# Weights written as pairs of keys in two halves of a row, and 32-column squares read at every second column, in a one-core hybrid attention layer

## The chip, the core and the metric

The kernel runs on one core of a Trainium2 chip. The metric is the device time of one execution in microseconds (us); lower is better. Three timed executions of the kernel before gave 795.85, 797.52 and 797.86 us, so the median is 797.52 us. The profile is of a fourth execution, which took 796.99 us.

## What is computed

One layer of a streaming encoder, for a prompt of 1024 tokens and a sample of 32 tokens that share all weights. Of the reference, cut to what matters here:

```python
u = rmsnorm(h, g_pre) @ w_in                     # qA kA vA gA qB kB vB gB, 512 columns each
oA = band_attention(...)                         # 8 heads x 64, softmax over own 64-frame chunk and 8 before
oB = stick_breaking(...)                         # 8 heads x 64, strictly causal
y  = concat(oA * silu(gA), oB * silu(gB)) @ w_out
h  = h + rmsnorm(y, g_post)
h  = h + sigmoid(h @ w_ple_gate) * (p @ w_ple)

# band attention:        s = q k^T * scale + bias;  w = softmax(s);  o = w v
# stick breaking:        z = q k^T * scale
#   log_1m = log_sigmoid(-z) (causal);  after = sum of log_1m over later keys
#   w = exp(log_sigmoid(z) + after);    o = w v
```

Both attentions make a matrix of weights with queries in the 128 partitions and keys along the row. The product with the values needs it the other way round, with keys in the partitions. How the weights are turned is what the change touches.

## The kernel before

**Stages.** The 16 heads are taken in pairs of heads, in the order A0 B0 A1 B1 A2 B2 A3 B3 (`pairs`). While the attention of one pair runs, the projections of the next are woven between its steps, and during B3 the eight gate projections. After the attention come two 1024-wide products (output and gate), done with a seven-product scheme. All matrix products are split in high and low parts (`hi`, `lo`).

**Order.** All operations are first recorded, then a planner (`Recorder.plan`) sets the order on each engine from modelled costs, and `emit` (line 497, which is why every row of the profile says L497) issues them. Each engine then executes its own queue strictly in that order: TensorE (PE), VectorE (DVE), ScalarE (ACT), GpSimd (POOL), and SyncE (SP), which issues all DMAs.

**A head, block by block.** A head has eight query blocks of 128 (`i` = 0 to 7). `scores(i)` multiplies q and k into PSUM (tile `SA` or `SB`). In band attention (A), VectorE adds the bias and takes the row's extreme (`om<-SA,biasA`, with its result in `statA`), then ScalarE takes the exponential with the row sum (`be<-om,statA`, followed by a short accumulator read into `sums`). In stick breaking (B), ScalarE takes a sigmoid (`om<-SB`), VectorE scans it (`om<-om,SB`), and GpSimd subtracts neighbours (`be<-om`). `om` and `be` are two ring buffers in SBUF. So the weights `be` have two producers: **ScalarE's exponential in A, GpSimd's difference in B**.

**Turning the weights.** Most blocks are small and are turned on TensorE (`ptw`). The blocks in the table `ROUND` go another way: A blocks 4, 5, 6, 7 (640 keys each) and B blocks 4, 5, 6 (640, 768, 896 keys), 4 x 8 + 3 x 8 = 56 in all. For them, `weights_t` has VectorE turn 32x32 squares (`STREAM_TRANSPOSE om<-be`), then one DMA writes the row to DRAM (`swapA<-om`, `swapB<-om`) and one brings it back turned (`be<-swapA`, `be<-swapB`). ScalarE then makes the high part (`wTh<-be`) and VectorE the low part (`wTl<-be,wTh`).

For this, the key of a square's row has to be dealt out by four: the producer's helper `apart` (line 872) writes key 4k + c of each 128-key block to column 32c + k, so that consecutive results are written 32 columns apart, and one square is 32 consecutive columns. The values are turned in a like way in `values_out` (line 731), which reads every second column of its source: `vxA<-stvA`, `vxB<-stvB`, 128x1024 each. `keys_out` turns the keys from consecutive columns (`ktB<-stkB`, 128x1024).

**Row sums.** After A's block 7, VectorE inverts the eight sums (`sumsA<-sumsA`), TensorE turns them (`ptsA<-ident,sumsA`) and ScalarE copies them out (`sumrowA`). This transpose stands at a fixed place in TensorE's queue, and whatever is behind it there waits until block 7's exponential is done.

Of the kernel before, what the change touches and what calls it, by code (L numbers as in the profile page):

```python
# [13 lines left out]
P = 128  # L14
# [28 lines left out]
def f(ap):  # L43

    return ap.bitcast(F32)
# [457 lines left out]
def stream_step(  # L503
# [7 lines left out]
    nc = rec  # L511
# [8 lines left out]
    def psum(tag, name):  # L520
        return ps.tile([P, 512], F32, tag=tag, name=name, bufs=PS_BUFS[tag])

    def scratch(shape, name):
        return Buf(shape, F32, name=name, real=dram.tile(shape, F32, tag=name, name=name))
# [28 lines left out]
        out=maskb, in_=maskb, pattern=[[-1, P]], base=0, channel_multiplier=1,  # L553
# [282 lines left out]
    def attention(ab, p, h):  # L836
# [14 lines left out]
        def lo_block(i):  # L851
            return max(0, i - 4) if ab == "A" else 0
# [4 lines left out]
        def cost(i):  # L857
            return i + 1 - lo_block(i)
# [13 lines left out]
        def apart(i, x, out=False):  # L872

            if i not in together:
                return x
            return x.rearrange("p (b c k) -> p b k c" if out else "p (b k c) -> p b k c", c=4, k=32)

        def scores(i):
            L, kd, kl = Lq[h], KDh[h], KLD[h]
# [13 lines left out]
            if ab == "B":  # L893
                a, b, s = pieces[-1]
                dg = s[:, b - a - P:b - a]
                nc.vector.tensor_tensor(dg, dg, maskb, ALU.add)
                nc.gpsimd.memset(w0[:, n:n + 1], 1.0)
                for a, b, s in pieces:
                    nc.scalar.activation(w0[:, a:b], s, AF.Sigmoid, scale=-1.0)
                for a, b, s in reversed(pieces):  # L900
                    rev = w0[:, a:b][:, ::-1]
                    nc.vector.tensor_tensor_scan(rev, rev, s, w0[:, b:b + 1], ALU.mult, ALU.bypass)
                nc.gpsimd.tensor_tensor(apart(i, w1[:, 0:n], True), apart(i, w0[:, 1:n + 1]), apart(i, w0[:, 0:n]), ALU.subtract)
            else:
                m = small.tile([P, 4], F32, tag="stat", name=f"stat{nm}_{i}", bufs=6)
                sums = box["sums"]
                for j, (a, b, s) in enumerate(pieces):
                    nc.vector.tensor_tensor_reduce(
                        w0[:, a:b], s, box["bias"][:, n - b:n - a][:, ::-1], 1.0,
                        3e38 if j == 0 else m[:, j - 1:j], ALU.add, ALU.min, m[:, j:j + 1])  # L910
                last = len(pieces) - 1
                nc.scalar.activation(apart(i, w1[:, 0:n], True), apart(i, w0[:, 0:n]), AF.Exp, bias=m[:, last:last + 1], scale=-1.0, accum_out=sums[:, i:i + 1])
                if i == 7:
                    nc.vector.reciprocal(sums, sums)
                    pt = psum("T", f"pts{nm}")
                    nc.tensor.transpose(pt[0:8, 0:P], sums, ident)
                    row = at.tile([P, 4 * P], F32, tag="ot", name=f"sumrow{nm}", bufs=2)[0:8, 0:P]
                    nc.scalar.copy(row, pt[0:8, 0:P])
                    dma(rs_dr[2 * p + h, 0:SEQ].rearrange("(i q) -> i q", q=P), row)
# [8 lines left out]
        def weights_t(i):  # L928
            g = i // 4
            step, size = LAID[ab, g]  # L930
            if g not in wT:
                wT[g] = [x.tile([P, size * P], f"{x.name}{nm}_{g}") for x in (ringh, ringl)]
            b0 = lo_block(i)
            w0, w1 = state.pop(i)
            n = i + 1 - b0
            at_ = ((i - 4 * g) * step + b0) * P
            hi, lo = (x[:, at_:at_ + n * P] for x in wT[g])
            if i in together:

                group = together[i]  # L940
                done_with.append((i, hi, lo))
                if i != group[-1]:
                    return
                w0, w1 = whole[group]
                m = sum(cost(x) for x in group)
                first = {x: sum(cost(y) for y in group[:k]) for k, x in enumerate(group)}
                squares = w0[:, 0:m * P].rearrange("p (c b q) -> p b c q", c=4, q=32)
                for x, _, _ in done_with:
                    y = slice(first[x], first[x] + cost(x))
                    nc.vector.transpose(squares[:, y], w1[:, y.start * P:y.stop * P])  # L950
                dr = scratch([4, P, m * 32], f"swap{nm}_{i}")
                dma(dr.rearrange("g (k c) x -> (g k) (c x)", c=4), w0[:, 0:m * P])
                dma(w1.rearrange("p (g x) -> p g x", g=4), dr.rearrange("g p x -> p g x"))
                turned = w1.rearrange("p (g b q) -> p g b q", g=4, q=32)
                for x, hi, lo in done_with:
                    src = turned[:, :, first[x]:first[x] + cost(x), :]
                    hi, lo = (y.rearrange("p (b g q) -> p g b q", g=4, q=32) for y in (hi, lo))
                    nc.scalar.copy(hi, src)
                    nc.vector.tensor_tensor(lo, src, f(hi), ALU.subtract)
                done_with.clear()  # L960
                return
            for b in range(0, n, 4):
                m = min(4, n - b)
                pt = psum("T", f"ptw{nm}_{i}_{b}")
                for x in range(m):
                    nc.tensor.transpose(pt[:, x * P:(x + 1) * P], w1[:, (b + x) * P:(b + x + 1) * P], ident)
                c = slice(b * P, (b + m) * P)
                nc.scalar.copy(hi[:, c], pt[:, 0:m * P])
                nc.vector.tensor_tensor(lo[:, c], pt[:, 0:m * P], f(hi[:, c]), ALU.subtract)
# [25 lines left out]
        out = {("B",): (0.0, begin)}  # L995
        for i in range(8):
            out["S", i] = (0.107 * cost(i) + SPACE_S, lambda i=i: scores(i))
            out["T", i] = (0.107 * cost(i) + SPACE_T, lambda i=i: weights_t(i))
# [255 lines left out]
    for n in range(-1, 8):  # L1254
        a = len(order)
        if n < 7:
            ab, p = pairs[n + 1]
# [458 lines left out]
    def short_product(nm, left, q):  # L1716
        o1, o2, both, minus = left
        acc = psum("S", f"{nm}8_{q}")[0:2 * NS]
        todo = ((o1, "B11"), (o2, "B21")) if q == 0 else ((both, "B22"), (minus, "T3"))
        i = 0  # L1720
        for a, key in todo:
            for kt in range(KT):
                for part in range(2):
                    nc.tensor.matmul(acc, a[:, kt, :], blocks[nm, key][:, part, kt, :], start=(i == 0), stop=(i == 4 * KT - 1))
                    i += 1
        y = at2.tile([P, 512], F32, tag="bias", name=f"{nm}j8_{q}", bufs=2)
        nc.scalar.copy(y[0:NS], acc[NS:2 * NS])
        nc.vector.tensor_tensor(y[0:NS], acc[0:NS], y[0:NS], ALU.add)
        return y[0:NS]
# [31 lines left out]
    for m, (nm, src, group) in enumerate(sets):  # L1761
        last_set = m == len(sets) - 1
        state = [{}, {}]
        for n, prod in enumerate(ORDER):
            for pair, t in enumerate(group):
# [29 lines left out]
                b = blocks[nm, WHICH[prod]]  # L1795
# [70 lines left out]
        if m in (0, 2):  # L1866
            if m == 0:
                row = Row(8, fb.tile([P, D], F32, tag="GP", name="h1_8"))
                row.load()
                for q in range(2):  # L1870
                    y = short_product(nm, short, q)
# [3 lines left out]
            else:  # L1875
                for q in range(2):
                    g8 = Gate(8, HALF[q])
                    y = short_product(nm, short, q)
# [38 lines left out]
```

## Time and profile before

| | |
|---|---|
| three timed executions | 795.85, 797.52, 797.86 us |
| median | 797.52 us |
| profiled execution | 796.99 us |
| its span, from the first to the last instruction | 795.20 us |
| mean granted TensorE clock | 0.997 |
| DMA | 177.83 MB, 224 GB/s |

The profile's rows name engine, operation, output tile <- input tiles, shapes and count. "Idle before" is the time that the engine stood still before an instruction, with what ended it. The attention lies at about 64 to 560 us of the span: A0 to about 110, B0 to 185, A1 to 233, B1 to 320, A2 to 350, B2 to 437, A3 to 470, B3 after that. The output products take the time from 600 us on, where nothing is turned through `swap`.

### The profile page before, as it was taken

The page shows a single profiled execution, that of the slowest core. Times are in us where ns is not written, and L with a number is a line of the kernel's source. Part 1 is how long each engine was busy: PE and PEld are TensorE (multiplying, and loading weights), DVE is VectorE, ACT ScalarE, POOL GpSimd, SP SyncE. Part 2 cuts the span into 40 slices and gives each one's busy share as a digit, 9 for nine tenths or more (in the row PEclk, how much of TensorE's full clock was granted, in tenths as well). Part 3 has the DMA queues.
Part 4 walks back from the last instruction along what each step waited for, and adds up shares of the span by engine and source line. Part 5 has one row for each costly group of instructions (what it writes and reads, how often), then busy time and mean ns, then how long its engine had stood idle before and what let it go on. Part 6 is the DMA issues. An engine that isn't in the chain of part 4 may idle for free. (4 is left out here: it accounts for less than half of the span.)

```text
span 795.2 us, 13848 instructions
## 1 busy us (share of the span) xinstructions
PE 772.9 (97%) x4518; PEld 709.4 (89%) x4518; DVE 600.3 (75%) x1007; ACT 519.7 (65%) x1039; POOL 447.9 (56%) x503
## 2 busy tenths in 40 slices
PE   8999999999999999999999999999999999999997
PEld 6999989998999999889999888999997877888786
DVE  6716788897889985799899788985446878686655
ACT  5636686577696644896567786542349867876741
POOL 5624638883556876234652327788634358597613
PEclk9999999999999999999999999999999999999999
DMA  8519998778988869776557668884769857569734
GB/s 268 164 45 288 247 280 284 236 222 295 252 261 261 261 196 258 213 214 204 136 161 169 204 203 259 255 241 142 229 228 336 276 172 269 202 228 314 230 110 133
DMA packets 176330, 177.83 MB, mean 224 GB/s; under 512 B 38129, under 2 KB 132057, under 8 KB 176258
## 3 DMA queue, kind: packets, MB, share of 16 engines
q1 hardware_dynamic: 176258, 176.95, 73.6%
q8 instruction: 36, 0.59, 0.3%
q14 instruction: 36, 0.29, 0.1%
HBM read 107.62 MB, written 60.88 MB: 212 GB/s over the span
## 5 line engine op out<-in xcount | busy, mean ns | idle before, releaser
L497 POOL TENSOR_TENSOR be<-om 128x128 f32<-128x128 f32 (+7 forms) x64 | 84.0, 1324 | 57.2 <-DVE om L497 10.5
L497 DVE TENSOR_TENSOR_SCAN om<-om,SB 128x384 f32<-128x384 f32 (+5 forms) x96 | 94.3, 999 | 9.9 <-ACT om L497 5.0
L497 ACT ACTIVATE be<-om,statA 128x640 f32<-128x640 f32 (+4 forms) x64 | 63.9, 1021 | 9.6 <-DVE wTl L497 4.2
L497 DVE TENSOR_TENSOR wTl<-be,wTh 128x640 fp32r<-128x640 f32 (+2 forms) x56 | 62.2, 1115 | 10.6 <-ACT wTh L497 10.4
L497 DVE STREAM_TRANSPOSE om<-be 128x640 f32<-128x640 f32 (+2 forms) x56 | 49.6, 888 | 11.4 <-ACT be L497 8.0
L497 ACT ACTIVATE om<-SB 128x384 f32<-128x384 f32 (+5 forms) x96 | 44.7, 491 | 20.2 <-DVE SB L497 9.8
L497 ACT CAST wTh<-be 128x640 fp32r<-128x640 f32 (+2 forms) x56 | 43.3, 774 | 12.7 <-DMA be<-swapB 7.0
L497 POOL TENSOR_TENSOR oB<-oB,oB 128x256 f32<-128x256 f32 x32 | 26.8, 862 | 15.0 <-DMA oB<-in_w_out_dram 14.8
L497 DVE CUSTOM_DVE_ANT_0 om<-SA,biasA 128x320 f32<-128x320 f32 (+2 forms) x64 | 29.7, 482 | 7.0 <-PE SA L497 5.2
L497 POOL TENSOR_TENSOR gB<-gB,gB 128x256 f32<-128x256 f32 x32 | 28.3, 902 | 11.9 <-DMA gB<-in_w_ple_gate_dram 10.8
L497 POOL TENSOR_TENSOR klB<-stkB,kdB 64x1024 fp32r<-64x1024 f32 x8 | 19.4, 2426 | 26.7 <-ACT kdB L497 25.6
L497 PE MATMUL SB<-kdB,LB 128*128 128x384 f32 (+5 forms) x96 | 33.5, 351 | 0.7 <-DVE om L497 0.7
L497 ACT CAST wTh<-ptwB 128x512 fp32r<-128x512 f32 (+3 forms) x48 | 22.2, 482 | 17.7 <-PE ptwB L497 15.8
L497 PE MATMUL SB<-klB,LB 128*128 128x384 f32 (+5 forms) x96 | 32.9, 347 | 0.0
L497 PE MATMUL SA<-kdA,LA 128*128 128x320 f32 (+2 forms) x96 | 30.1, 323 | 0.9 <-DVE statA L497 0.7
L497 DVE TENSOR_TENSOR wTl<-ptwB,wTh 128x512 fp32r<-128x512 f32 (+3 forms) x48 | 25.2, 542 | 5.9 <-ACT wTh L497 4.5
L497 PE MATMUL SA<-klA,LA 128*128 128x320 f32 (+2 forms) x96 | 29.3, 317 | 0.2 <-DMA klA<-klA 0.2
L497 POOL TENSOR_TENSOR sggA<-sggA,oggA 128x352 f32<-128x352 f32 x24 | 25.7, 1075 | 6.4 <-DVE sggA L497 2.3
L497 POOL TENSOR_TENSOR klA<-stkA,kdA 64x1024 fp32r<-64x1024 f32 x8 | 20.9, 2608 | 6.9 <-ACT kdA L497 6.5
L497 PE MATMUL PVB<-wTh,v2B 128*128 128x512 f32 (+1 forms) x96 | 21.6, 349 | 2.8 <-DVE otA L497 1.9
L497 POOL TENSOR_TENSOR h<-h,x 128x512 f32<-128x512 f32 (+1 forms) x18 | 23.6, 1337 | 0.0
L497 POOL TENSOR_TENSOR sggB<-sggB,oggB 128x352 f32<-128x352 f32 x12 | 11.9, 988 | 20.3 <-DVE sggB L497 15.7
(707 smaller groups left out, 2630.7 us busy)
## 6 DMA issues: line engine op xcount, KB each, us to landing
swapA<-om SPq DMA_DIRECT2D x32, 320.0 KB, 4.3
be<-swapA SPq DMA_DIRECT2D x32, 320.0 KB, 4.8
oB<-in_w_out_dram SPq DMA_DIRECT2D x16, 256.0 KB, 5.2
sum_dro<-oB SPq DMA_DIRECT2D x16, 256.0 KB, 4.0
gB<-in_w_ple_gate_dram SPq DMA_DIRECT2D x16, 256.0 KB, 4.6
sum_drg<-gB SPq DMA_DIRECT2D x16, 256.0 KB, 4.7
x<-in_x_prompt_dram SPq DMA_DIRECT2D x16, 256.0 KB, 3.5
h_dr<-h SPq DMA_DIRECT2D x8, 512.0 KB, 3.9
```

Source lines behind the costliest of these rows:

```text
L497: getattr(getattr(tc.nc, o.what[0]), o.what[1])(*args, **kw)
```

## The change

```diff
@@ -873,7 +873,7 @@  def apart(i, x, out=False):
             if i not in together:
                 return x
-            return x.rearrange("p (b c k) -> p b k c" if out else "p (b k c) -> p b k c", c=4, k=32)
+            return x.rearrange("p (c k d) -> p k c d" if out else "p (k c d) -> p k c d", c=2, d=2)
@@ -944,10 +944,10 @@  def weights_t(i):
                 first = {x: sum(cost(y) for y in group[:k]) for k, x in enumerate(group)}
-                squares = w0[:, 0:m * P].rearrange("p (c b q) -> p b c q", c=4, q=32)
+                squares = w0[:, 0:m * P].rearrange("p (i j b q) -> p i j b q", i=2, j=2, q=32)
                 for x, _, _ in done_with:
                     y = slice(first[x], first[x] + cost(x))
-                    nc.vector.transpose(squares[:, y], w1[:, y.start * P:y.stop * P])
+                    nc.vector.transpose(squares[:, :, :, y], w1[:, y.start * P:y.stop * P].rearrange("p (i b k j) -> p i j b k", i=2, k=32, j=2))
                 dr = scratch([4, P, m * 32], f"swap{nm}_{i}")
                 dma(dr.rearrange("g (k c) x -> (g k) (c x)", c=4), w0[:, 0:m * P])
                 dma(w1.rearrange("p (g x) -> p g x", g=4), dr.rearrange("g p x -> p g x"))
```

The producer now writes keys 4k and 4k + 1 side by side in the first half of the row and 4k + 2 and 4k + 3 side by side in the second half: of every four results two go to adjacent columns, then two to adjacent columns half a row further on. A 32x32 square is then every second column of 64 (half `i`, parity `j`, block `b`), and the squares are written one behind the other instead of dealt out over four quarters. The row that leaves for DRAM is the same, element for element, and both DMAs are unchanged.

No instruction is added, removed or moved: on all five engines the queues hold the same instructions in the same order, and SyncE's and TensorE's rows are the same throughout. Only access patterns differ.

On ScalarE, in the first A head (tiles `be` and `om` are the ring buffers, `statA_4` to `statA_7` belong to blocks 4 to 7, `sumsA_230` is the head's tile of row sums), before:

```order
L497 ACTIVATE be,sumsA_230<-om,statA_4_235 128x5x32x4
L497 COPY wTh<-ptwA_1_0_987 128x256
L497 COPY LA_1007<-stqA_413 64x1024
L497 COPY stkB_1028<-mm_kB_0_866 128x352
L497 ACTIVATE be,sumsA_230<-om,statA_5_236 128x5x32x4
L497 ACTIVATE be,sumsA_230<-om,statA_6_949 128x5x32x4
L497 COPY wTh<-ptwA_2_0_988 128x384
L497 COPY wTh<-ptwA_3_0_1030 128x512
L497 ACTIVATE be,sumsA_230<-om,statA_7_956 128x5x32x4
```

and now:

```order
L497 ACTIVATE be,sumsA_230<-om,statA_4_235 128x160x2x2
L497 COPY wTh<-ptwA_1_0_987 128x256
L497 COPY LA_1007<-stqA_413 64x1024
L497 COPY stkB_1028<-mm_kB_0_866 128x352
L497 ACTIVATE be,sumsA_230<-om,statA_5_236 128x160x2x2
L497 ACTIVATE be,sumsA_230<-om,statA_6_949 128x160x2x2
L497 COPY wTh<-ptwA_2_0_988 128x384
L497 COPY wTh<-ptwA_3_0_1030 128x512
L497 ACTIVATE be,sumsA_230<-om,statA_7_956 128x160x2x2
```

Four exponentials have another shape of the same 640 elements; none has moved past another instruction.

On VectorE, at the end of the same head, around the inversion of the sums:

```order
 L497 ISA statA_7_956 128x1
-L497 STREAM_TRANSPOSE om<-be 128x5x4x32
+L497 STREAM_TRANSPOSE om<-be 128x640
 L497 TENSOR_TENSOR wTl<-ptwA_2_0_988,wTh 128x384
 L497 TENSOR_TENSOR wTl<-ptwA_3_0_1030,wTh 128x512
 L497 RECIPROCAL sumsA_230<-sumsA_230 128x8
-L497 STREAM_TRANSPOSE om<-be 128x5x4x32 x3
+L497 STREAM_TRANSPOSE om<-be 128x640 x3
```

Each square transpose now writes one plain run of 640 columns; its place relative to the inversion is as before.

## The prediction

> **What bounds the kernel now.** I read the busy times first, then the same by stage, then who TensorE waits for.
>
> ```profile
> PE 772.9 (97%) x4518; PEld 709.4 (89%) x4518; DVE 600.3 (75%) x1007; ACT 519.7 (65%) x1039; POOL 447.9 (56%) x503
> ```
>
> TensorE is busy for 772.9 of 795.2 us. Its instructions are untouched, so a faster ScalarE can only win from the other 22.3 us. By stage (columns: stretch, its length, then busy us and instructions of PE, PEld, DVE, ACT and POOL, the clock granted, DMA share, GB/s), A0 B0 A1 B1 A2 B2 A3 B3:
>
> ```profile
> 64.00:110.00 46.00, 43.07 (x275) 41.36 (x275) 33.24 (x77) 34.34 (x69) 17.89 (x19) 1.00 1.01 271
> 110.00:185.00 75.00, 74.78 (x467) 71.87 (x466) 68.54 (x106) 50.35 (x101) 59.63 (x68) 1.00 0.82 256
> 185.00:233.00 48.00, 46.50 (x308) 45.13 (x307) 38.73 (x81) 37.11 (x72) 21.87 (x31) 1.00 0.92 268
> 233.00:320.00 87.00, 85.31 (x536) 81.43 (x536) 71.40 (x112) 54.23 (x113) 62.23 (x71) 1.00 0.86 247
> 320.00:350.00 30.00, 27.55 (x175) 25.51 (x174) 24.86 (x59) 27.86 (x56) 6.26 (x9) 1.00 0.73 215
> 350.00:437.00 87.00, 86.78 (x548) 83.92 (x548) 80.74 (x122) 59.00 (x115) 43.64 (x44) 1.00 0.64 172
> 437.00:470.00 33.00, 30.96 (x198) 28.58 (x196) 26.89 (x64) 28.44 (x55) 8.53 (x14) 1.00 0.62 184
> 470.00:560.00 90.00, 87.79 (x548) 85.79 (x549) 67.47 (x98) 44.17 (x98) 67.12 (x72) 0.98 0.78 235
> ```
>
> TensorE stands still for 2.93 + 1.50 + 2.45 + 2.04 = 8.9 us in the four A stages and 0.22 + 1.69 + 0.22 + 2.21 = 4.3 us in the four B stages. In A2, ScalarE is busy for 27.86 of 30 us: there it is the fuller of the two helpers. In B0 and B2 it is VectorE, at 91 and 93%. What ends TensorE's waits (total us, times, longest):
>
> ```profile
> PE ptsA L497 <- DVE sumsA L497: 5.2, 7, 1.5
> PE PVB L497 <- DVE otA L497: 1.9, 1, 1.9
> PE ptkB L497 <- ACT stkB L497: 1.1, 1, 1.1
> PE PVB L497 <- ACT wTh L497: 0.9, 1, 0.9
> PE SB L497 <- DVE om L497: 0.7, 2, 0.5
> PE PVA L497 <- ACT wTh L497: 0.6, 2, 0.3
> PE SsA L497 <- ACT QsA L497: 0.5, 1, 0.5
> PE ptwA L497 <- ACT sumrowA L497: 0.5, 1, 0.5
> PE ptosA L497 <- ACT be L497: 0.4, 1, 0.4
> ```
>
> The largest, 5.2 us in seven waits, is the transpose of A's row sums, waiting for VectorE's inversion. The end of head two shows what is behind that:
>
> ```profile
> 104.64 1.48 ACT L497 ACTIVATE be<-om,statA 128x640 f32<-128x640 f32 x1
> 105.97 1.46 ACT L497 ACTIVATE be<-om,statA 128x640 f32<-128x640 f32 x1
> 107.28 1.43 ACT L497 ACTIVATE be<-om,statA 128x640 f32<-128x640 f32 x1
> 108.75 0.20 DVE L497 RECIPROCAL sumsA<-sumsA 128x8 f32<-128x8 f32 x1 [0.43 <-ACT be L497]
> 109.10 0.27 PE L497 MATMUL ptsA<-ident,sumsA 128*8 128x128 f32 x1 [0.92 <-DVE sumsA L497]
> ```
>
> Three exponentials run end to end on ScalarE; when the last is done VectorE, already idle for 0.43 us, inverts, and TensorE, idle for 0.92 us, goes on. So the exponential's length sets TensorE's wait here, and these are exactly the instructions whose writing changes.
>
> **The change part by part.** The prices by shape (busy us, mean ns of one):
>
> ```profile
> L497 ACT ACTIVATE be<-om,statA 128x640 f32<-128x640 f32 x32 | 46.1, 1481 | 1.1 <-PE ptwA L497 1.1
> L497 ACT ACTIVATE be<-om,statA 128x512 f32<-128x512 f32 x8 | 5.8, 722 | 1.2 <-DVE wTl L497 1.1
> L497 ACT ACTIVATE be<-om,statA 128x384 f32<-128x384 f32 x8 | 4.9, 613 | 3.1 <-DVE wTl L497 3.1
> L497 DVE STREAM_TRANSPOSE om<-be 128x640 f32<-128x640 f32 x40 | 33.0, 829 | 8.9 <-ACT be L497 8.0 <-POOL be L497 0.8
> L497 DVE STREAM_TRANSPOSE om<-be 128x896 f32<-128x896 f32 x8 | 8.8, 1105 | 1.5 <-POOL be L497 1.2 <-POOL om L497 0.3
> L497 DVE STREAM_TRANSPOSE om<-be 128x768 f32<-128x768 f32 x8 | 7.7, 966 | 1.0 <-POOL om L497 0.9
> L497 DVE STREAM_TRANSPOSE ktB<-stkB 128x1024 f32<-128x1024 f32 x4 | 5.0, 1238 | 2.5 <-ACT stkB L497 2.5
> L497 DVE STREAM_TRANSPOSE vxB<-stvB 128x1024 f32<-128x1024 f32 x4 | 4.9, 1235 | 0.1
> L497 POOL TENSOR_TENSOR be<-om 128x1024 f32<-128x1024 f32 x8 | 18.2, 2270 | 5.3 <-ACT QsB L497 1.5 <-DVE om L497 1.3 <-ACT QfsB L497 1.3
> L497 POOL TENSOR_TENSOR be<-om 128x896 f32<-128x896 f32 x8 | 15.6, 1944 | 9.7 <-ACT om L497 2.4 <-DMA swapB<-om 2.1 <-DVE newl L497 1.9
> L497 POOL TENSOR_TENSOR be<-om 128x640 f32<-128x640 f32 x8 | 12.2, 1530 | 7.0 <-DVE om L497 3.1 <-ACT wTh L497 2.3 <-DVE wTl L497 1.6
> L497 POOL TENSOR_TENSOR be<-om 128x512 f32<-128x512 f32 x8 | 8.8, 1098 | 11.1 <-DVE wTl L497 5.3 <-issue 2.4 <-DVE om L497 2.1
> ```
>
> *ScalarE's exponentials.* Blocks 2 and 3 (384 and 512 columns) write plain runs: (722 - 613) / 128 = 0.85 ns a column. At that rate 640 columns would take 722 + 128 x 0.85 = 831 ns. The scattered ones take 1481, so 650 ns of each, 1.0 ns a column, is the price of writing single words 32 columns apart. No row shows a pair-wise write by ScalarE. The bounds are 1481 (a pair is no better than a single word) and 831 (pairs are free); halfway, one penalty for each pair, is 1156. The step that is paid for is the hop to another place for every element, and half the elements now make no hop, so I exclude a loss. I take 850 ns, near the lower bound: 32 x 0.63 = 20 us off ScalarE, 5 us in each A stage.
>
> [...]
>
> *VectorE's squares.* 56 transposes now read every second column. The values' transpose already reads that way (`vxB`, 1235 ns for 1024 columns), and the keys' reads consecutive columns (`ktB`, 1238). So the reading costs nothing, and I take 829 ns for 640 columns as now. The output becomes one plain run, as `ktB`'s is; by `ktB`, 1238 x 640 / 1024 = 774 ns would be the lower bound. The upper bound is the only surcharge for hopping single words in the trace, ScalarE's 1.0 ns a column, or 650 ns.
>
> [...]
>
> *GpSimd's differences.* Plain ones take 1098 ns (512) and 2270 (1024), so 640 and 896 columns come to 1391 and 1977 by the line between them, against 1530 and 1944 scattered: -139 and +33 ns, no sign of a price for scattering. I take zero; the bounds are 0.14 us either way for each of 24, or 3.4 us of an engine that is 56% busy.
>
> *DMAs* keep bytes, patterns and places in SP's queue: zero. They only start earlier, behind earlier squares.
>
> *What reaches the end.* Each A head has four such exponentials in its queue before the inversion, so up to 2.5 us can be gained against waits of 1.5 us at most. Of the 5.2 us I take 4.6 and not all: VectorE was idle for only 0.43 us before the inversion above, so it can come forward by more only where VectorE's earlier work, itself behind exponentials, comes forward too. The other waits that end on ScalarE within A stages, PVA 0.6, SsA 0.5, ptwA 0.5, ptosA 0.4, make 2.0; I take half, 1.0, since copies and other exponentials stand in them as well. Then TensorE comes to the B stages about 5.6 us earlier in all, where VectorE is over 90% full and no faster. The waits that end there (PVB 1.9 and 0.9, ptkB 1.1, SB 0.7) sum to 4.6 us, and I let them grow by a third, 1.5. Sum: 4.6 + 1.0 - 1.5 = 4.1 us. The profiled execution took 796.99 us, 1.79 more than its span, and is 0.5 under the median of 797.52. Against that median: **793.4 us**.
>
> **Rivals.** *One: pairs cost ScalarE nearly as much as single words.* The exponential stays over 1.3 us, at most 6 us come off ScalarE, and about a quarter of the 5.6 us is won: 1.0, so 796.5. For it: no pair-wise write in the trace. Against it: half the hops are gone.
>
> *Two: the gain is taken back.* Exponentials fall to 0.85 us, but TensorE, ahead after each A stage, waits as much longer in the next B stage, for VectorE (68.54 of 75 us) or a DMA. For it: those fractions, and 1.9 us of PVB's wait that stems from values returning by DMA. Against it: VectorE's own work in A was also held up by the exponentials (8.0 us idle before the squares, ended by ACT be), so it comes to B earlier too. Left is 1 us: 796.5.
>
> *Three, the slower side: longer waits cost clock as well.* One wait of 1.93 us does so now:
>
> ```profile
> 494.00:496.00 2.00, 0.26 (x2) 0.00 (x0) 1.97 (x3) 1.95 (x6) 1.31 (x2) 1.00 1.05 289
> 496.00:498.00 2.00, 1.81 (x6) 1.62 (x7) 1.97 (x3) 0.43 (x1) 0.63 (x1) 0.58 1.08 251
> 498.00:500.00 2.00, 2.00 (x13) 2.00 (x12) 1.59 (x4) 0.95 (x2) 1.67 (x2) 0.57 0.87 228
> ```
>
> TensorE does nothing for most of two microseconds, and then gets 0.58 and 0.57 of its clock: 2 x 0.42 + 2 x 0.43 = 1.7 us lost on top. The 1.5 us wait in A0 cost no clock (1.00 in that row). So a wait decides from somewhere between 1.5 and 1.9 us on. If the earlier TensorE meets two more such waits behind transfers that don't come earlier, they cost 2 x (1.9 + 1.7) = 7.2, and less the 4.1 gained that is 3.1 us slower: 800.6. For it: the DMA engines' share of 1.05 there. Against it: only one wait of the attention is that long now. The same mechanism could also win 3.6 us if this wait falls away, which bounds the gain: 4.1 + 3.6 = 7.7, or 789.8.
>
> *Four: the squares slow down*, by 1.0 ns a column: 40 x 0.65 + 8 x 0.78 + 8 x 0.91 = 39.5 us on VectorE, of which nearly half is in B stages where it has 6.5 us free in 75. A gain of nothing in A, and a quarter of the sum on TensorE's path: 10 us, so 807.5. Against it: the 1235 ns of `vxB`.
>
> **How the numbers follow.** Forecast 0.55, rival one 0.12, two 0.18, three 0.09, four 0.06. The forecast's own range is 789.8 (the last bound) to 796. With rivals one and two, and measuring within 0.3% (2.4 us, about what this kernel's measurement tells from no change), the range is 789.3 to 798.8; it leaves out rivals three and four and little else. Faster by over 0.3% (under 795.1) has nearly all of the forecast and a part of two: 0.57. Rivals one and two give most of "within 0.3%": 0.27. Three and four, and a mishap beside them, give slower: 0.16.
>
> **What would show it.** The row of A's exponentials at 128x640: 0.85 us is the forecast, over 1.3 rival one. The squares' rows: 0.83, 0.97 and 1.1 us (640, 768, 896 columns) as now, else rival four. TensorE's wait for `sumsA`: from 5.2 us to under 1. If that holds and the span has not fallen by 3 us or more, the waits in the B rows have grown, which is rival two, and a clock under 1.00 in more rows of the attention is rival three. The prediction is wrong if the exponentials fall and the wait for `sumsA` does not.

## The result, and the profile after

The changed kernel takes 788.94 us (median of 787.92, 788.35, 789.54 and 790.08), beside 797.41 us for the kernel before on the same chip: a ratio of 0.989, with a 95% interval of 0.987 to 0.991. In a second comparison, below, it is 0.992 (0.990 to 0.995). So it is 6 to 9 us faster. The forecast was 793.4 us, 4.1 us faster; the direction was right, the gain is about one and a half times to twice as large, and the measured time lies just below the lowest time that the prediction allowed for (789.3 us).

The costliest groups by shape, of the kernel after (busy us, mean ns of one, idle time before them and what ended it):

```profile
L497 ACT ACTIVATE be<-om,statA 128x640 f32<-128x640 f32 x32 | 28.4, 893 | 1.1 <-DVE statA L497 1.1
L497 POOL TENSOR_TENSOR be<-om 128x896 f32<-128x896 f32 x8 | 13.9, 1733 | 7.4 <-DMA wr_gB<-in_w_in_dram 2.4 <-DMA swapB<-om 2.1 <-DVE om L497 1.7
L497 POOL TENSOR_TENSOR be<-om 128x640 f32<-128x640 f32 x8 | 11.1, 1387 | 7.1 <-DVE om L497 3.1 <-ACT wTh L497 2.3 <-DVE wTl L497 1.7
L497 DVE STREAM_TRANSPOSE om<-be 128x640 f32<-128x640 f32 x40 | 32.9, 827 | 1.8 <-ACT be L497 0.8 <-POOL be L497 0.6
L497 DVE STREAM_TRANSPOSE om<-be 128x896 f32<-128x896 f32 x8 | 8.8, 1102 | 0.9 <-POOL be L497 0.8
L497 DVE STREAM_TRANSPOSE om<-be 128x768 f32<-128x768 f32 x8 | 7.7, 966 | 0.7 <-POOL om L497 0.5
```

ScalarE's exponential fell from 1481 to 893 ns. GpSimd's differences fell too, which was not forecast: 1530 to 1387 ns for 640 columns and 1944 to 1733 for 896 columns. VectorE's squares take what they took, 827 for 829 ns, though they read every second column; their idle time behind ScalarE fell from 8.0 to 0.8 us.

The eight stages again, in the same windows (the later ones hold work of up to 8 us further on in the program):

```profile
64.00:110.00 46.00, 43.65 (x277) 41.42 (x276) 32.84 (x81) 31.99 (x68) 18.49 (x20) 1.00 1.01 268
110.00:185.00 75.00, 75.00 (x468) 71.95 (x467) 68.24 (x104) 49.42 (x101) 58.75 (x68) 1.00 0.82 256
185.00:233.00 48.00, 48.00 (x320) 47.02 (x319) 38.86 (x81) 37.15 (x78) 22.79 (x33) 1.00 0.95 285
233.00:320.00 87.00, 84.85 (x536) 81.34 (x535) 72.11 (x114) 53.56 (x114) 59.87 (x70) 1.00 0.87 244
320.00:350.00 30.00, 29.52 (x194) 28.40 (x193) 27.84 (x62) 26.76 (x58) 9.94 (x13) 1.00 0.79 229
350.00:437.00 87.00, 86.22 (x545) 83.27 (x545) 77.65 (x121) 56.80 (x117) 39.87 (x45) 1.00 0.65 180
437.00:470.00 33.00, 32.78 (x217) 31.42 (x216) 29.08 (x65) 28.32 (x58) 12.32 (x18) 1.00 0.67 202
470.00:560.00 90.00, 88.49 (x553) 85.60 (x552) 65.42 (x97) 40.25 (x86) 65.38 (x70) 1.00 0.76 231
```

TensorE's standing time, stage length less busy time, is 2.35 + 0 + 0.48 + 0.22 = 3.0 us in the A stages, where it was 8.9, and 0 + 2.15 + 0.78 + 1.51 = 4.4 us in the B stages, where it was 4.3. So A won 5.9 us and B gave nothing back. (With the stages cut at the same TensorE instructions in both kernels, in place of the same times, it is 9.2 to 3.6 us in A and 4.1 to 3.9 us in B.) The last stage's clock is 1.00 where it was 0.98. TensorE's waits, the longest groups in the attention:

```profile
PE SA L497 <- DVE statA L497: 1.6, 3, 1.2
PE PVB L497 <- ACT wTh L497: 1.2, 2, 0.6
PE ptwA L497 <- ACT be L497: 0.9, 2, 0.5
PE SsA L497 <- ACT QsA L497: 0.8, 1, 0.8
PE SA L497 <- DMA klA<-klA: 0.7, 1, 0.7
```

The 5.2 us for the row sums are gone from the list altogether, as are, in this execution, the waits for stkB (1.1), for SB (0.7) and for otA (1.9). At the end of head two, the timeline of the kernel after reads (start and length in us first):

```profile
104.67 0.90 ACT L497 ACTIVATE be<-om,statA 128x640 f32<-128x640 f32 x1
105.54 0.88 ACT L497 ACTIVATE be<-om,statA 128x640 f32<-128x640 f32 x1
106.40 0.88 ACT L497 ACTIVATE be<-om,statA 128x640 f32<-128x640 f32 x1
107.54 0.16 DVE L497 RECIPROCAL sumsA<-sumsA 128x8 f32<-128x8 f32 x1
108.48 0.27 PE L497 MATMUL ptsA<-ident,sumsA 128*8 128x128 f32 x1
```

The exponentials now follow each other every 0.87 us, where it was every 1.31 (105.97 to 107.28). One overlaps the next, so by these rows 0.44 us of the queue is saved for each and not the 0.59 by which the mean fell: 32 x 0.44 = 14 us in all. ScalarE's busy time agrees, with 506.1 us for 519.7. The inversion is done 0.8 us before TensorE asks for it, and TensorE no longer waits.

### The profile page after: what moved, and what is told of

It reads as the page before. It is cut to its first block, busy times and chain, and to the rows that moved or that the text cites. A ratio compares the mean times of both kernels' runs of the same rounds, so it can differ in the third digit from the quotient of the medians.

```text
span 786.1 us, 13848 instructions
## 1 busy us (share of the span) xinstructions
PE 771.0 (98%) x4518; PEld 708.7 (90%) x4518; DVE 597.3 (76%) x1007; ACT 506.1 (64%) x1039; POOL 445.5 (57%) x503
## 5 line engine op out<-in xcount | busy, mean ns | idle before, releaser
L497 POOL TENSOR_TENSOR be<-om 128x128 f32<-128x128 f32 (+7 forms) x64 | 79.7, 1252 | 53.1 <-DVE om L497 12.9
L497 ACT ACTIVATE be<-om,statA 128x640 f32<-128x640 f32 (+4 forms) x64 | 46.2, 727 | 8.9 <-DVE statA L497 4.6
L497 POOL TENSOR_TENSOR gB<-gB,gB 128x256 f32<-128x256 f32 x32 | 27.5, 878 | 14.1 <-DMA gB<-in_w_ple_gate_dram 12.9
L497 POOL TENSOR_TENSOR sggB<-sggB,oggB 128x352 f32<-128x352 f32 x12 | 12.9, 1074 | 19.8 <-DVE sggB L497 15.2
```

What stands on the lines that cost most here:

```text
L497: getattr(getattr(tc.nc, o.what[0]), o.what[1])(*args, **kw)
```

## The experiments

All kernels of a group ran on the same chip beside runs of the kernel before; ratios are to those, with 95% intervals. "Exponential" is the mean of A's 32 exponentials of 640 columns. "Standing" is TensorE's standing time over the same stretch, 64 to 560 us, of that kernel's one profiled execution; it was 13.3 us before and is 7.5 us after. The profiled executions of e2 and e9 were the slowest of their twelve.

| kernel | ratio | interval | exponential, ns | standing, us |
|---|---|---|---|---|
| e1_a_only | 0.991 | 0.989 to 0.994 | 895 | 9.3 |
| e2_b_only | 1.000 | 0.998 to 1.002 | 1476 | 19.0 |
| e3_singles | 1.001 | 0.999 to 1.004 | 1467 | 14.1 |
| e4_plain | 0.991 | 0.988 to 0.994 | 828 | 9.2 |
| e5_before_no_sums | 1.001 | 0.999 to 1.003 | 1486 | 16.4 |
| e6_after_no_sums | 0.990 | 0.987 to 0.993 | 895 | 8.0 |
| e7_block7 | 0.998 | 0.996 to 1.000 | 1338 | 14.6 |
| e8_before_again | - | - | 1487 | 14.2 |
| e9_load_a | 0.998 | 0.996 to 1.000 | 898 | 12.1 |
| e10_load_b | 1.002 | 0.999 to 1.004 | 893 | 15.8 |
| e11_after_again | 0.992 | 0.990 to 0.995 | 892 | 9.4 |
| e12_plan_1481_before | 1.002 | 1.000 to 1.004 | 1493 | 14.6 |
| e13_plan_1481_after | 1.000 | 0.998 to 1.002 | 896 | 14.1 |
| e14_load_b_planned | 1.002 | 1.000 to 1.004 | 899 | 11.3 |
| e15_plan_893 | 1.002 | 1.000 to 1.004 | 901 | 14.5 |
| e16_plan_1160 | 1.001 | 0.999 to 1.003 | 895 | 12.8 |

### Which producer: e1 and e2

```diff
+        new = ab == "A"          # e2: ab == "B"
...
+            if new:
+                return x.rearrange("p (c k d) -> p k c d" if out else "p (k c d) -> p k c d", c=2, d=2)
             return x.rearrange("p (b c k) -> p b k c" if out else "p (b k c) -> p b k c", c=4, k=32)
```

The squares are read in the way that matches.

> Pairs only in the band attention (ScalarE's exponentials, 32 blocks); stick breaking (GpSimd's differences) as before. Theory 'exponentials': the whole gain is ScalarE's, so about 788.9 us, with the exponential of 640 columns at 0.89 us, the wait for sumsA near 0 and the wait of 1.9 us with the half clock near 490 us gone. Theory 'both producers' (GpSimd's differences also fell, 1530 to 1387 ns, 1751 to 1575, 1944 to 1733, 4.2 us in all): about 791 to 792, with 2 to 3 us of the gain missing.

> Pairs only in stick breaking (GpSimd's differences, 24 blocks); the exponentials as before at 1.48 us. Theory 'exponentials': 797.0 to 797.4, no difference that can be measured. Theory 'both producers': 794 to 795, and GpSimd's rows at 1387, 1575 and 1733 ns as in the changed kernel.

With pairs in A alone the gain is there (0.991); with pairs in B alone there is none (1.000, interval 0.998 to 1.002). GpSimd's rows fell in e2 as in the changed kernel, to 1385, 1573 and 1732 ns, and that is worth nothing that could be measured. The theory "exponentials" holds, "both producers" falls.

### What makes the write cheap: e3 and e4

```diff
-            return x.rearrange("p (c k d) -> p k c d" if out else "p (k c d) -> p k c d", c=2, d=2)
+            return x.rearrange("p (c k) -> p k c" if out else "p (k c) -> p k c", c=2)     # e3
+            return x                                                                      # e4
```

In e3 the squares' view is also changed from `(i j b q)` to `(j i b q)`.

> Every second key goes to the second half of the row, as single words (key 2k + c to column c n/2 + k), the squares again every second column with their two indices exchanged. Theory 'run length' (two adjacent words are what makes the write cheap): the exponential stays at 1.3 us or more and the time at 795 or more. Theory 'hop' (two streams, each going forward, are what makes it cheap, or the distance): 0.9 us and about 789.

> The producers write plain rows, so the keys of a square aren't dealt out and the turned weights are of the wrong keys; everything else as in the changed kernel. Exponential at 0.83 us (0.06 under pairs). If exponentials are still what TensorE waits for in the band attention, 1 to 2 us faster than the changed kernel (787 to 788); if pairs have taken all there is, equal to it within 1 us (788 to 790).

The exponential's group, first of e3, then of e4:

```profile
L497 ACT ACTIVATE be<-om,statA 128x640 f32<-128x640 f32 x32 | 45.6, 1467 | 1.1 <-PE ptwA L497 1.1
```

```profile
L497 ACT ACTIVATE be<-om,statA 128x640 f32<-128x640 f32 x32 | 26.4, 828 | 1.1 <-PE ptwA L497 1.1
```

Single words in two streams, each going steadily forward, cost 1467 ns, no less than single words 32 columns apart (1481). Runs of two cost 893 and a plain row 828. So the run of two words is what makes this exponential's write cheap, and neither the distance nor the number of streams. e3's squares read every second column as the changed kernel's do, so that reading isn't what won the time either. The plain row is 65 ns shorter still, but at 0.991 (0.988 to 0.994) the kernel's time can't be told from that with pairs.

### The wait for the row sums: e5 and e6

```diff
+        for o in ops:
+            if o.eng == "PE" and o.what[1] == "transpose" and o.args[1].buf.name.startswith("sums"):
+                o.args = (o.args[0], o.args[2][:, 0:8], o.args[2])
```

This stands in `emit` behind the ordering, so every queue is as before.

> The kernel before, in which the transpose of A's row sums turns eight columns of the identity instead of the sums, so that TensorE does the same work at the same place and waits for no inversion; the prompt's band attention is divided by wrong sums. Exponentials stay at 1.48 us. Theory 'row sums': TensorE's 5.2 to 5.7 us of waiting for sumsA are most of what the change won, so about 5 us faster than before (ratio about 0.994); what stays is the wait for stkB (1.1), for SB (0.7) and for ptosA (0.4). Rival 'next in line': ScalarE is as late as ever, so TensorE waits as long at the next instruction that needs it, and at most 2 us are won (ratio over 0.997).

> The changed kernel with the same replacement in the transpose of the row sums (same wrong sums). Theory 'row sums': the wait is gone there already, so the same time as the changed kernel (ratio to before 0.989, within 0.002). If the row sums still held anything up, faster than that by over 2 us.

This was the forecast's main step, and it falls. The wait for the sums is gone from e5's list, but the kernel is not faster (1.001). e6 is at 0.990, beside 0.989 and 0.992 for the changed kernel. The timeline of e5 at the end of head two shows why:

```profile
109.01 1.48 ACT L500 ACTIVATE be<-om,statA 128x640 f32<-128x640 f32 x1
109.75 0.27 PE L500 MATMUL ptsA<-ident 128*8 128x128 f32 x1
110.94 0.58 ACT L500 COPY otA<-PVA 64x512 f32<-64x512 f32 x1
111.55 0.68 DVE L500 TENSOR_TENSOR otA<-PVA,otA 64x512 f32<-64x512 f32 x1
112.29 0.86 PE L500 MATMUL PVA<-wTh,v2A 128*128 128x512 f32 x4 [0.97 <-DVE otA L500]
```

The transpose no longer waits and runs while the last exponential is still going. But otA's copy stands behind that exponential in ScalarE's queue, VectorE's sum behind the copy, and TensorE waits for it for 0.97 us, where it had waited for 0.92 before. ScalarE is as late as it was, and the next instruction to need it pays. The rival "next in line" holds.

### How much of it: e7, and a second profile of before

e7 writes pairs only in block 7 of each A head (`if ab == "A" and i == 7` in place of `if new`).

> Pairs only in block 7 of each A head, the last of four scattered exponentials before the inversion; blocks 4 to 6 of A and all of B as before. Theory 'queue' (each exponential of the four adds its 0.59 us to how late the inversion is): of the waits 1.50, 0.92, 0.18, 0.25, 1.21, 0.24, 0.87 at most 0.59 each goes, so the wait for sumsA falls from 5.2 to about 2.1 us, and the gain is 3 to 4 us (ratio about 0.996). Rival 'last one only' (the earlier three are hidden behind other work): the wait falls under 0.7 us and the gain is nearly the whole of 8 us (ratio under 0.992).

> The kernel before, unchanged, for a second profile. If its wait of 1.9 us for otA with the half clock behind it (near 490 us) belongs to the kernel, it is there again; if it was chance in one execution's transfers, it is absent or elsewhere, and the waits for sumsA (5.2), stkB (1.1) and SB (0.7) are there again within 0.6.

A quarter of the exponentials being short gives a ratio of 0.998 (0.996 to 1.000), about a quarter of the gain. That is less than either theory expected; "last one only" falls, and 0.996 lies at the edge of the interval. The wait for the sums in e7:

```profile
PE ptsA L497 <- DVE sumsA L497: 2.7, 4, 1.0
```

It fell from 5.2 to 2.7 us, near the 2.1 expected, which fits that each exponential adds its part to how late the queue is. The waits of e8, the kernel before in another execution of 792.4 us span:

```profile
PE ptsA L497 <- DVE sumsA L497: 4.9, 6, 1.5
PE SA L497 <- DVE statA L497: 1.9, 3, 1.1
PE SsB L497 <- ACT QsB L497: 1.7, 1, 1.7
PE SsA L497 <- ACT QsA L497: 1.6, 1, 1.6
PE ptkB L497 <- ACT stkB L497: 1.1, 1, 1.1
```

Sums (4.9) and stkB (1.1) are there again; the 1.9 us for otA with the half clock behind it is not. It did not belong to the kernel, but to the execution that the prediction was made from.

### ScalarE's time put back: e9, e10, and the changed kernel again

```diff
+                name = o.args[0].buf.name if o.eng == "ACT" else ""
+                if name.startswith("beA") and AF.Exp in o.args and int(name[-1]) < 4:      # e10: "omB", AF.Sigmoid
+                    for _ in range(3):
+                        tc.nc.scalar.copy(self.load.get(), self.load.get())
```

Also in `emit`, so that all else keeps its order. The lines that make the tile `load` and fill it are left out here.

> The changed kernel with idle work on ScalarE: three copies of 8 columns (about 0.6 us together) behind the exponential of each of blocks 0 to 3 of every A head, 32 times; the exponentials of blocks 4 to 7 stay short, and all else keeps its order. Theory 'ScalarE's time' (TensorE in the A stages goes at the pace of ScalarE's queue, and 8.5 of 18.8 us saved reach the end, 0.45 of each): the 19 us put back cost 7 to 9 us, ratio to before 0.997 to 1.001. Rival 'length of one exponential' (what counts is the way from a block's scores to its squares and sums): those are as short as in the changed kernel, so ratio 0.988 to 0.993.

> The same idle work, 32 times three copies, behind the first sigmoid of blocks 0 to 3 of every B head. Theory 'ScalarE's time': in B stages ScalarE is busy for 49 to 57 of 75 to 87 us and VectorE is the fuller one, so it is hidden: at most 2 us slower than the changed kernel, ratio 0.988 to 0.992. Rival 'ScalarE everywhere' (its time counts in any stage of the attention): as dear as in A, ratio 0.996 or more.

> The changed kernel, unchanged, beside the two above: ratio 0.987 to 0.991, and its second profile tells which of its waits come again: none for sumsA, and none for otA of 1.9 us with half a clock behind it.

ScalarE's busy time goes from 505.4 us (e11) to 519.9 in both, about what the kernel before had (519.7). e11 is at 0.992, beside the 0.987 to 0.991 expected, again without a wait for sumsA or otA, but with a stretch of half clock of its own (last section). In A the idle work takes most of the gain away (0.998 for 0.992), although the dealt-out exponentials stay short: time in ScalarE's queue counts by itself, whatever the length of the single exponential. In B it takes all of it (1.002), which I had not expected, since ScalarE is busy there for two thirds of the time at most. A smaller part is clock: by the mean granted clock, the timed executions of e9 and e10 lost 2.1 and 2.2 us, those of e11 0.8 (one less the granted share, times the span). e10's waits:

```profile
PE PVB L497 <- ACT wTh L497: 2.7, 3, 1.3
PE ptvB L497 <- ACT stvB L497: 2.0, 1, 2.0
PE mm_vA L497 <- ACT wh_vA L497: 1.1, 1, 1.1
PE mm_kA L497 <- ACT stvB L497: 1.0, 1, 1.0
```

Those are 6.8 us on ScalarE's ordinary copies, where the changed kernel has 1.4 (1.2 for `PVB`, 0.2 for `ptvB`). The copies that the last three rows wait for, 4.1 us, stand in ScalarE's queue close behind idle copies. So ScalarE's average share in a stage doesn't tell whether its time is free: its idle time lies where it waits for others, and its results are wanted right away.

### The order of the queues: e12 to e16

In e12 (with the slow write) and e13, e15, e16 (with pairs) the planner's cost of a dealt-out exponential is raised from 846 ns, and every queue is ordered anew; e14 has e10's idle work as recorded operations.

```diff
-            return (90 if psum else 125) + 0.83 * n + (190 if "accum_out" in kw else 0), 105
+            dealt = 635 if "accum_out" in kw and len(out.shape) == 4 else 0      # e15: 47, e16: 314
+            return (90 if psum else 125) + 0.83 * n + (190 if "accum_out" in kw else 0) + dealt, 105
```

> The kernel before, but the planner's cost of a dealt-out exponential of 640 columns is raised from 846 ns (what a plain row would take) to 1481 ns, which is what it takes there; all engines' queues are ordered anew by that. Theory 'plan' (the order on record was made for 846 ns; what the change won is that the chip came to agree with the plan): a plan that knows the true length wins most of it back, ratio to before 0.990 to 0.995. Rival 'ScalarE's time' (each us on ScalarE costs 0.45 us at the end whatever the plan): 0.997 to 1.002.

> The changed kernel, in the order of the run above (planned for 1481 ns, while the exponentials take 893). Theory 'plan': a plan that is off in this direction costs something too, and the run is no faster than the one above by more than 3 us (within 0.004 in ratio). Rival 'ScalarE's time': it is faster than the one above by what the change won under the old plan, 7 to 8 us (0.009 to 0.010 in ratio).

> The changed kernel with the same idle work on ScalarE in the B heads as before (32 times three copies of 8 columns), but recorded as operations, so that the planner knows of their 0.2 us each and orders all queues around them. Theory 'plan': most of the 7 us that they cost unplanned is hidden, ratio 0.990 to 0.995. Rival 'ScalarE's time': as dear as unplanned, ratio 0.998 to 1.002.

> The changed kernel, with the planner's cost of the dealt-out exponential at 893 ns, what it takes on the chip now, in place of 846. Every queue is ordered anew. Theory 'plan' (what counts is that plan and chip agree): the agreement is as good as in the changed kernel or better, ratio 0.986 to 0.993. Rival 'this one order' (the order on record is a better one than the planner's next, and any reordering gives up more than the change won): ratio 0.997 to 1.003, and the three runs with other orders say nothing against ScalarE's time as such.

> The same for a planned 1160 ns, halfway to what it took before. Theory 'plan': between the changed kernel and the run planned for 1481 ns, ratio 0.993 to 0.998. Rival 'this one order': 0.997 to 1.003, no trend with the planned length.

e12 and e13 met one expectation of each theory and missed one of each: a plan with the true length did not help the slow kernel (1.002), and the short exponentials won only 0.002 in that order, within the noise. e15 shows that this can't be laid to a mismatch in the exponential's length: planned with 893 ns, what the chip takes, the changed kernel is at 1.002. In e14 the planned idle work cost as much as the unplanned. All five reordered kernels lie at 1.000 to 1.002. That is no fixed price of a new order, since the slow write lost only 0.002 by it in e12; in the new orders the short exponentials win next to nothing. These runs therefore say nothing against ScalarE's time in the order on record; they do show that the gain belongs to that order.

A part of the reason is the clock. The mean granted clock of the timed executions is 0.993 to 0.995 in the five reordered kernels and 0.999 in the kernel before beside them; reckoned as above, they lost 3.8 to 5.3 us to it and the kernel before 0.8 to 1.1. By the clock of their stages, the five profiles lost 3.4 to 3.7 us to it in the attention (0.96 over the 87 us of B1 in e13, e14 and e15; 0.96 over A1 and 0.98 over B1 in e12; 0.98 over B1 and 0.95 over A3 in e16); the kernel after lost none (1.00 in every stage), and e11 1.7. What makes up the rest was not found.

## Where the prediction was right and where it failed

**ScalarE's price: right.** 850 ns was taken, 893 measured. That pairs would come near the lower bound was my estimate, as no row of the profile before shows such a write. Rival one (over 1.3 us) did not come. The lower bound of 831 ns was the plain row's 828 in e4. What was missed is that consecutive exponentials overlap, so that 14 us of ScalarE's queue were saved and not 20.

**VectorE's squares: right.** 829 ns was taken, 827 measured, and rival four fell: reading every second column cost this transpose nothing. For ScalarE's write the run of words did count: 893 ns for pairs beside 828 for a plain row and 1467 for single words.

**GpSimd's differences: the price was wrong, its effect right.** Zero was taken from a line through two plain rows, although the scattered row of 640 columns, 1530 against 1391 ns, already showed a price. The line also put a plain row of 896 columns at 1977 ns; e4's takes 1730, and 1384 for 640, so the scattered ones had paid 214 and 146 ns each. e2 (1.000) shows no gain from that at the end.

**"Of the 5.2 us I take 4.6": the size came near, the mechanism did not, so the size was in part luck.** 5.9 us were won in the A stages where 4.6 + 1.0 were forecast. But all of the 5.2 us went. The 1.0 from other waits did not come: the rows PVA, SsA and ptwA hold 2.6 us after, and with ptosA they held 2.0 before. And 1.1 us more came from stkB, which the forecast had counted in B (next paragraph). The chain that I had followed, exponential to inversion to TensorE, was only where ScalarE's lateness showed; e5 took that wait away and won nothing.

**"I let them grow by a third, 1.5": this is the step that failed.** The waits in the B stages did not grow (4.4 us for 4.3). One of those counted, stkB (1.1), was no wait of a B stage: TensorE stands there at 197.3 us, inside A1. It and SB (0.7) are the same in all four profiles of this order with only slow exponentials in A (before, e8, e2, e3), and 0 to 0.6 and 0 to 0.5 in the five with short ones (after, e11, e1, e4, e6). So they shrink when ScalarE is less late; that SB's is lateness carried over from A is likely, not shown. Without this term the forecast would have been 5.6 us, at the edge of the 6 to 9 measured.

What was still missing lies in A. With the stages cut at the same TensorE instructions, the A stages last 157.8 us together in the mean of those four profiles and 150.3 in the mean of the five, the B stages 339.0 and 338.3. So A won 7.5 us and not 5.6, and with B it makes 8.2, within the 6 to 9 measured. Of A's, 6.3 us is standing time, and why TensorE's rows there are shorter by the rest is open.

**The execution that the prediction was made from.** Its wait of 1.9 us and half clock, which bounded the gain in rival three, are absent in a second execution (e8). But its standing time of 13.3 us was on the low side: e8, e2 and e3, all with the slow exponential, show 14.2, 19.0 and 14.1, while e11, e1, e4 and e6 show 8.0 to 9.4. The means of these, with before and after, are 15.2 and 8.7, or 6.5 us apart, which fits the measured gain. In these profiles other long waits come and go, and more with the slow ScalarE.

**Rival two** (taken back in B) did not happen in this order. In the reordered kernels nothing was won, in part because of the clock. **Rival three**'s point of decision, a wait between 1.5 and 1.9 us, was wrong as well: here no length of one wait decides (last section).

## What to carry to other kernels

When ScalarE writes single words with a step (1467 ns and more for 640 columns here), try two neighbours at a time (893 here); VectorE's square transpose undid that at no cost (827 ns for 829). When the longest wait in the list ends on an engine that works through a long queue in order, take the wait for a symptom: ask what else stands behind the same queue, since removing that one wait only hands it to the next instruction. And an engine's share of a stage doesn't show whether its time is free; idle work of known length, put into its queue with the order kept, tells more.

## What the runs showed of the hardware

The clock fell to half after waits of which none was long. In e11, the changed kernel again, it was so for 3.4 us, with no wait of TensorE in the attention over 1.2 us:

```profile
98.00:100.00 2.00, 1.81 (x12) 1.52 (x10) 2.00 (x6) 1.55 (x4) 0.00 (x0) 1.00 1.14 192
100.00:102.00 2.00, 0.82 (x5) 0.58 (x5) 1.20 (x3) 1.06 (x3) 1.75 (x2) 1.00 1.09 278
102.00:104.00 2.00, 1.64 (x7) 1.60 (x8) 1.27 (x2) 2.00 (x5) 0.48 (x1) 0.76 1.04 373
104.00:106.00 2.00, 2.00 (x8) 2.00 (x8) 1.89 (x3) 2.00 (x5) 0.00 (x0) 0.50 1.09 252
106.00:108.00 2.00, 2.00 (x12) 1.84 (x12) 1.87 (x4) 1.49 (x5) 0.00 (x0) 0.89 1.10 145
```

TensorE stood for 0.19 + 1.18 + 0.36 = 1.7 us within six, and the clock then fell to 0.50. Of the last three rows 0.24, 0.50 and 0.11 of the clock are lost, 1.7 us in all, which is 3.4 us at half the clock; the kernel before lost as much behind its wait of 1.93 us (0.58 and 0.57). In e8 a single wait of 1.7 us (the SsB row above) left the clock at 1.00:

```profile
504.00:506.00 2.00, 0.31 (x2) 0.23 (x2) 2.00 (x2) 0.41 (x1) 2.00 (x2) 1.00 0.88 283
506.00:508.00 2.00, 2.00 (x15) 1.98 (x15) 1.61 (x3) 0.00 (x0) 1.33 (x1) 1.00 0.91 258
508.00:510.00 2.00, 2.00 (x17) 2.00 (x16) 1.15 (x2) 1.77 (x4) 1.14 (x5) 1.00 1.04 289
```

Single waits of 1.8 us in e2 (SsA, with 1.00 in every stage of the attention), 2.0 us in e10 (ptvB, with 1.00 in all four B stages) and 2.2 us in e12 (mm_gA, with 1.00 in B3) cost no clock either. So the length of one wait does not decide. What does, these runs don't show.

ScalarE's exponential writes 640 columns in 828 ns as a plain row (e4), 893 to 895 in pairs (after, e1, e6) and 1467 to 1487 in single words (e3, before, e2, e5, e8); GpSimd's differences take 1384, 1387 and 1514 to 1530 ns for the same three in the kernels before and after, e3 and e4; VectorE's square transpose takes 825 to 830 ns in these four.
